# A seven-product pair for the first layer's last down chunks, and a new chunk order in the second mixer (Trainium2, one core)

## The chip, the cores and the metric

The kernel runs on one core of one Trainium2 chip. The metric is the device time of one execution in microseconds. The core's engines are TensorE (PE, with its weight loads as PEld), VectorE (DVE), ScalarE (ACT), GpSimd (POOL) and SyncE (SP), which here issues nearly all DMAs.

## The reference

A trunk of two layers on 256 tokens of width 2048 in float32. Each layer adds a token mixer and a gated MLP to the residual `h`, each behind an RMSNorm; a final RMSNorm closes it. Layer 0 mixes with a bidirectional mLSTM (8 heads), layer 1 with a bidirectional HGRN2 recurrence (16 heads of 128).

```python
for layer in range(DEPTH):
    hn = rmsnorm(h, norm_mix_g[layer])
    mix = mlstm_mixer(...) if layer % 2 == 0 else hgrn_mixer(...)
    h = h + mix
    h = h + conv_glu(rmsnorm(h, norm_ffn_g[layer]), ...)
return rmsnorm(h, final_g)

def conv_glu(hn, w_up, conv_w, conv_b, w_down):      # D_FF = 5504
    a, v = jnp.split(hn @ w_up, 2, axis=-1)
    c = conv_b + sum(ap[:, j:j + s] * conv_w[j] for j in range(3))   # ap: a padded by 1
    return (jax.nn.gelu(c, approximate=False) * v) @ w_down

# hgrn_mixer: q, i (the values V), g (the output gate), f_f, f_b = split(hn @ w_in)
```

## The kernel before

**Products.** Every float32 weight and activation is split into a high part, cast by ACT (L144), and a low part, subtracted by DVE (L145); each product is three matmuls (high by high, high by low, low by high). `split_weights` (L118) yields split pieces of 1024 weight columns; `stream` (L301) keeps three pieces ahead of the matmuls (`LOOK`).

**Chunks.** The kernel's work on PE is one list of `Chunk`s (L106), streamed in order. An "fm" chunk computes 256 features, features on the partitions (matmuls L340 of 512 columns and L344 of 256 for each k tile and half); `swap` exchanges the places of a 256-wide matmul and the 512-wide one behind it. A "tm" chunk computes 512 features with tokens on the partitions (six 512-wide matmuls of L356 for each k tile of 128). An "st" chunk is a **pair**: two 512-wide chunks of the down projection (or of a mixer's output projection) at once. It goes through its k tiles two at a time, a couple `u`. A couple plainly takes 2 x 2 x 2 products of 128x512, that is 24 matmuls (`squares_by_seven`, L214; all its matmuls are L231). A couple in `ch.seven` takes seven products, 21 matmuls, in the manner of Strassen: for this DVE forms three combinations T2, T3, T4 of the weight blocks and four sums of the token blocks (`token_sums`, L524). The pair uses all eight PSUM banks: four "mm" banks (pool psm) for the products that more than one block needs (P1, P6, P7, P5), four "aux" banks (pool psa) for the blocks themselves. After the last couple with seven, `mid` (L553 to L565) adds P1, P5, P6, P7 to the residual tile hm and so empties the psm banks; the couples behind it use the psa banks alone. `done` adds these at the end (four DVE adds).

**Weight combinations.** Those of a seven couple are either made when the piece is fetched (`combine`) or **stored**: `prepare` (L583) loads a couple's 1 MB as two 512 KB DMAs (`praw`), makes four DVE subtractions (L603), and stores it with two DMAs to DRAM (`tscr`). The pair later fetches 768 KB of the original (`raw`), 768 KB (`T`) and 256 KB from there. `prepare` runs as a side job during an earlier stage. `prepare_early` starts one in each mixer (`early[0]` in the first, period 19 for 8 items; `early[1]` in the second, period 26 for 15 items); each half of an FFN prepares others beside its up projection (`todo`). `ch.waits` holds a pair back, in program order, until its list of preparations is through.

**Order.** `Side` (L75) plans what runs beside the matmuls: generators that yield a delay in units of roughly a microsecond of PE work, which `stream` advances by `tick`. So the program order is fixed by hand when it is built: side jobs (preparation, norms, heads of the mixers) are put between the matmuls that tick past their due times. `late` issues a DMA on SP's queue pinned in program order.

**Stages.** Mixer 1 (`mlstm`), its output projection (`mixed`: a plain chunk, a pair with seven couples `SEVEN_MIX`, a plain chunk), FFN 0, mixer 2 (`hgrn`), its output projection, FFN 1. An FFN (`ffn`) goes in two parts of 22 and 21 feature tiles (FA, FB): up projection by "fm" chunks, gate and convolution by DVE and ACT, then the down projection of that part for all 2048 outputs, by two pairs. In part 0 both pairs have 8 seven couples (`SEVEN[0]`). In part 1 of layer 1 both have 7 (`SEVEN_END`). In part 1 of **layer 0** the first pair has 6 (`SEVEN[1]`), and the other two chunks are plain "tm" chunks (`project(...)[2:]`, weights `w_d2`).

**The seam.** While those plain chunks run, `Norm.add` and `Norm.turn` (L403 to L424) prepare the next norm: ACT squares each 512-wide quarter of hm, PE transposes it (L417, 16 transposes for the first two quarters) into an aux bank `pz`, and ACT and DVE split it into the activations `xt` (L362, L363). `turn` waits until no pair holds the banks (`held`). The last two quarters are turned after the last chunk. Then `hgrn` begins (`begin`, L938: the constant's DMA, the early preparation, small tables).

**Mixer 2.** For each quarter of 4 heads: three "fm" chunks, a V chunk ("tm"), three "fm" chunks, a G chunk ("tm", the output gate). A head's work (levels of products on ACT, DVE and POOL, then small PE products L1016, L1040, L1066) runs as a side job once its three "fm" results are there; it needs V for L1066, and its output needs G. V has one buffer.

Of the kernel before, what the change touches and what calls it, by code (L numbers as in the profile page):

```python
# [15 lines left out]
P = 128  # L16
# [30 lines left out]
LEAD = 48  # L47
TEMP = 3
GATES = 4 * AH
SEVEN = (1, 2, 3, 4, 6, 7, 8, 9), (1, 2, 4, 5, 7, 8)  # L50
SEVEN_END = (1, 2, 3, 4, 5, 6, 7)
END = 3
SCRATCH = 4096
SEVEN_MIX = (2, 4, 6)

QUAD = 32
LEVELS = (1, 2, 4, 8, 16, 32, 64)
FINE = 5
C_ID, C_MF, C_MB, C_SUM, C_LV = 0, 128, 384, 640, 768
# [1 line left out]


def trunk_kernel(ctx, tc, xT, x_d, fg_d, pp_d, cst_d, w_gate, w_first, w_aq, w_ak, w_av, w_ao, w_aout, w_ao2,
                 w_bq, w_bv, w_bg, w_bout, w_bo2, w_up, w_d0, w_d1, w_d2, w_d3, out, mscr, tscr):
    nc = tc.nc
    act, dve, pool, pe = nc.scalar, nc.vector, nc.gpsimd, nc.tensor

# [115 lines left out]
    def split_squares(ch, parts):  # L183

        units, raws, kept = (ch.nk + 1) // 2, {}, {}
        side.until(lambda: ch.waits is None or ch.waits)

        def raw(u):
            if u not in raws and u < units:
                n = 1536 if u in ch.stored else min(2048, 1024 * ch.nk - 2048 * u)  # L190
                raws[u] = load_raw(ch.src, 2048 * u, 2048 * u + n)
                if u in ch.stored:
                    kept[u] = temporary(ch.pool, "T")
                    nc.sync.dma_start(kept[u], ch.stored[u][:, 0:1536])
                    nc.sync.dma_start(raws[u][:, 1536:2048], ch.stored[u][:, 1536:2048])
            return raws.get(u)

        def combine(u):
            r, T = raw(u), temporary(ch.pool, "T")
            B11, B22, B21, B12 = (r[:, j * 512:(j + 1) * 512] for j in range(4))  # L200
            T2, T3, T4 = (T[:, j * 512:(j + 1) * 512] for j in range(3))
            for x, y, out in ((B12, B22, T3), (B12, B11, B12), (B22, B12, T2), (B21, T2, T4)):
                dve.tensor_tensor(out, x, y, ALU.subtract)
            kept[u] = T

        for u in range(units):
            r = raw(u)
            yield *parts(r[:, 0:1024], 1024, more=ch.pool), 1
            if u + 1 in ch.seven and u + 1 not in ch.stored:
                combine(u + 1)  # L210
            if u in ch.seven:
                yield *parts(kept[u][:, 0:1024], 1024, more=ch.pool), 1
            if 2 * u + 1 < ch.nk:
                yield *parts(r[:, 1024:2048], 1024, more=ch.pool), 1  # L214
            if u in ch.seven:
                yield *parts(kept[u][:, 1024:1536], 512, more=ch.pool), 1
# [4 lines left out]
    def squares_by_seven(ch, fetch, ready):  # L221
# [37 lines left out]
        for u in range(units):  # L259
# [27 lines left out]
            if u in ch.seven:  # L287
# [7 lines left out]
                products((C21, A22, T4))  # L295
                if u == last:
                    ch.mid(psm_)
                continue
            B21, B12 = piece()
            for ps, (x, w), (y, v) in ((C11, (A11, B11), (A12, B21)), (C12, (A11, B12), (A12, B22)),  # L300
# [80 lines left out]
    class Norm:  # L381
# [25 lines left out]

        def turn(self, c):
            yield 2.5
            while held:  # L410
                yield 1.0
            for k0 in (4 * c, 4 * c + 2):
                pz = aux("pz")
                for k in (k0, k0 + 1):
                    for t in range(2):
                        o = (k - k0) * T + t * P
                        pe.transpose(pz[:, o:o + P], hm[:, t, k * P:(k + 1) * P], ident)  # L417
                for k in (k0, k0 + 1):
                    self.take(k, pz[:, (k - k0) * T:(k - k0 + 1) * T])
                yield 1.0  # L420
# [127 lines left out]
    def pair(src, nk, c0, x, sums, norm, seven):  # L548
# [16 lines left out]
            pool.tensor_tensor(part(1, 1), part(1, 1), u, ALU.add)  # L565

        def done(ps):
            for i in range(4):
                h = part(i // 2, i % 2)
                dve.tensor_tensor(h, h, ps[i], ALU.add)  # L570
            if norm is not None:
                norm.add(c0)
                side.push(second())

        def second():
# [2 lines left out]

        ch = Chunk("st", src, nk, x, done)
        ch.mid, ch.seven, ch.sums = mid, seven, sums  # L580
        ch.stored, ch.waits, ch.pool = {}, None, None
        return ch

    def prepare(tiles, todo, first, period, finished, start, ahead):
# [66 lines left out]
    def mlstm(norm, nxt):  # L651
# [192 lines left out]
        for pr in range(AH // 2):  # L844
# [36 lines left out]
            def done_first(ps, done_v=done_v):  # L881
# [8 lines left out]
                norm.finish()  # L890
                done_v(ps, note)
                side.push(start(gs))
                prepare_early(box["mp"], 0, 45.0, 19.0)

            last = {}

# [32 lines left out]
    def hgrn(norm, nxt):  # L929
# [4 lines left out]
        def begin():  # L934
            mp = box["mp"] = stack.enter_context(tc.tile_pool(name="hg", bufs=1))
            late(cst[:, C_LV:], cst_d[:, C_LV:])
            prepare_early(mp, 1, 30.0, 26.0)
            box["turn"] = 0  # L938
            lb = box["lb"] = mp.tile([P, KT], F32, name="lb")
            oml = box["oml"] = mp.tile([P, KT], F32, name="oml")  # L940
# [147 lines left out]
                YT[hd] = slot(hd, "yb")  # L1088
                split(YT[hd], pz[:, 0:T], col("b_head_g", hd))

        swaps = {(0, 1): (0, 6), (1, 0): (2, 24), (1, 2): (4,), (2, 0): (2, 24), (2, 2): (4,), (3, 0): (2,), (3, 2): (10,)}
        heads = [dict() for _ in range(BH)]
        chunks = []
        for qd in range(BH // 4):
            four = dict()

# [5 lines left out]
            def done_g(ps, four=four, qd=qd):  # L1102
# [3 lines left out]
                    dve.scalar_tensor_tensor(sg[:, t], ps[t], norm.rc[:, t:t + 1], sg[:, t], ALU.mult, ALU.mult)  # L1106
                side.push(finish(qd, four))

            for i in range(6):
                if i == 3:  # L1110
                    chunks.append(Chunk("tm", w_bv[qd], KT, norm.x, done_v, paced=True))
                def done_i(ps, i=i, qd=qd):
                    for f in range(2):
                        r = 2 * i + f
                        take(4 * qd + r // 3, r % 3, ps[f])
                chunks.append(Chunk("fm", w_bq[6 * qd + i], KT, norm.x, done_i, begin if not chunks else None,
                                    swap=swaps.get((qd, i), (1, 13) if i == 3 else ()), paced=True))
            for j in range(4):
                heads[4 * qd + j]["qd"] = four
            chunks.append(Chunk("tm", w_bg[qd], KT, norm.x, done_g, paced=True))  # L1120

        def yx(k):
            side.until(lambda: YT[k] is not None)
# [5 lines left out]
    def ffn(layer, norm, nxt):  # L1129
        stack = ExitStack()  # L1130
        ending = isinstance(nxt, FinalNorm)
        seven = SEVEN[0], SEVEN_END if ending else SEVEN[1]
        box = dict(n=(2 * len(SEVEN[0]) + len(SEVEN[1])) * layer)
        chunks, pairs = [], []

        def begin():
# [7 lines left out]
        def done_up(f, i, GT, SX, seven):  # L1144
            def go(ps):
# [17 lines left out]
                GT.append(g)  # L1163
                if i % 2 and i // 2 in seven:
                    n = seven.index(i // 2)
                    if seven is not SEVEN[1]:
                        z = GT[i - 1][:, P:T], GT[i - 1][:, T + P:2 * T]
                    else:
                        if n % 3 == 0:
                            box["s4"] = mp.tile([P, 768], F32R, tag=f"sx{len(seven) + n // 3}", name="s4")  # L1170
                        z = tuple(box["s4"][:, (n % 3 * 2 + j) * P:(n % 3 * 2 + j + 1) * P] for j in range(2))
                    SX[i // 2] = token_sums(mp, n, box["c"], c, avc[:, 0:2 * T], z)
                box["c"] = c
            return go
# [1 line left out]
        for part, (f0, nf) in enumerate(((0, FA), (FA, FB))):  # L1176
# [7 lines left out]
                                  todo, 18.0, (nf * 10.4 - 26.0) / len(todo), finished, late, True))  # L1184

            for i in range(nf):
                chunks.append(Chunk("fm", w_up[layer, f0 + i], KT, norm.x, done_up(f0 + i, i, GT, SX, seven[part]),
                                    prep if i == 0 else None,
                                    swap=(2,) if part and i == 0 else (3,) if f0 + i == 1 else (), paced=True))
            def two(src, c0, norm, seven, todo=todo, finished=finished, GT=GT, SX=SX, nf=nf):  # L1190
                ch = pair(src, nf, c0, lambda k: GT[k], lambda u: SX[u], norm, seven)
                for u in seven:
                    ch.stored[u] = tscr[box["n"]]
                    todo.append((src[:, 2048 * u:2048 * (u + 1)], tscr[box["n"]]))
                    box["n"] += 1
                ch.waits, ch.pool = finished, None
                pairs.append(ch)
                return ch

            chunks.append(two(w_d0[layer][:, f0 * 1024:(f0 + nf) * 1024], 0, nxt if part else None, seven[part],  # L1200
                              *(() if part else early[layer])))
            if not part:
                chunks.append(two(w_d1[layer], 2, None, seven[0]))
            elif ending:
                chunks[-1].before = nxt.load
                chunks.append(two(w_d3, 2, None, seven[1], *early[layer]))
                chunks[-1].last, chunks[-1].half = True, nxt.half
            else:
                chunks += project(lambda c: w_d2[c % 2], nf, lambda k, GT=GT: GT[k], nxt)[2:]
        return chunks, stack.close  # L1210


# [54 lines left out]
def layout(x, norm_mix_g, norm_ffn_g, mlstm_w_in, mlstm_b_gate, mlstm_head_g, mlstm_w_out, hgrn_w_in, hgrn_lb,  # L1267
# [16 lines left out]
    def outer(w):  # L1284
# [21 lines left out]
        w_bv=_cols(wb[:, 2048:4096], 512), w_bg=_cols(wb[:, 4096:6144], 512),  # L1306
        w_up=np.ascontiguousarray(up).reshape(2, FT, P, KT * 256),
        w_d0=np.stack([squares(d[:, :, 0:2]) for d in down]), w_d1=np.stack([squares(d[:FA, :, 2:4]) for d in down]),
        w_d2=np.ascontiguousarray(down[0, FA:, :, 2:].transpose(2, 1, 0, 3)).reshape(2, P, FB * 512),
        w_d3=squares(down[1, FA:, :, 2:]),  # L1310
    )


def build(nc, ins, out_shape=(2, P, D), **kw):
# [1 line left out]
          for k, a in ins.items()}  # L1316
    out = nc.dram_tensor("out", out_shape, F32, kind="ExternalOutput").ap()
    mscr = nc.dram_tensor("mscr", (64, T), F32, kind="Internal").ap()
    tscr = nc.dram_tensor("tscr", (4 * len(SEVEN[0]) + len(SEVEN[1]) + 2 * len(SEVEN_END), P, 2048), F32, kind="Internal").ap()
    with tile.TileContext(nc, schedule_with_timeline_sim=True) as tc:  # L1320
        with ExitStack() as ctx:
            trunk_kernel(ctx, tc, ap["xT"], ap["x"], ap["fg"], ap["pp"], ap["cst"], ap["w_gate"], ap["w_first"],
                         ap["w_aq"], ap["w_ak"], ap["w_av"],
                         ap["w_ao"], ap["w_aout"], ap["w_ao2"], ap["w_bq"], ap["w_bv"], ap["w_bg"],
                         ap["w_bout"], ap["w_bo2"], ap["w_up"], ap["w_d0"], ap["w_d1"], ap["w_d2"], ap["w_d3"], out, mscr, tscr, **kw)


# [10 lines left out]
```

## Time and profile before

| | us |
| --- | --- |
| median of 3 runs | 2383.42 |
| lowest and highest | 2383.26, 2383.58 |
| the profiled run | 2384.87 |
| its span in the trace | 2382.9 |

The span runs from the first instruction to the last one's end; the run's time also holds what lies around it. Stages in the trace, in us from the span's start: mixer 1 to 303 and its output projection to 395; FFN 0 up to 637, its two pairs to 735, up to 979, the pair to 1032.5, the two plain chunks to 1092; mixer 2 to 1592 and its output projection to 1683; FFN 1 to 2373. In the rows a group is "line engine operation out<-in xcount"; in a timeline the first number is the start and the second the time from there to the end of the last of the group.

### The profile page before, as it was taken

How to read it: one execution, taken by the hardware profiler on the slowest of the kernel's cores; microseconds unless marked ns; L12 is line 12 of the kernel's file. 1: busy time of each engine (PE TensorE's matmuls, PEld its weight loads, DVE VectorE, ACT ScalarE, POOL GpSimd, SP SyncE). 2: the span in 40 equal slices, each digit the busy share in tenths (PEclk: the TensorE clock that was granted, in tenths of full speed). 3: DMA queues.
4: the chain of work that ended last, by engine and by line, in shares of the span. 5: the costliest groups of instructions: out<-in, count | busy, mean ns of one | idle time of the engine just before them, and what ended most of it. 6: DMA issues, size and time to landing. Idle time of an engine off the chain costs nothing.

```text
span 2382.9 us, 38182 instructions
## 1 busy us (share of the span) xinstructions
PE 2365.6 (99%) x14572; PEld 2024.3 (85%) x14572; DVE 1938.4 (81%) x3001; ACT 1433.6 (60%) x2271; POOL 205.4 (9%) x242
## 2 busy tenths in 40 slices
PE   9999999999999999999999999999999999999998
PEld 7888888888888888888888888887888888888886
DVE  7777687888788887766888888888788788888787
ACT  7655456555665555655666666665555566455565
POOL 0100000000000000001233222320000000000000
PEclk9999999999999999999999999999999999999999
DMA  8777656886697885755666666764788588887695
GB/s 300 240 272 268 227 174 214 302 303 226 223 354 272 283 280 195 274 190 204 244 234 228 246 236 227 245 225 173 258 299 283 195 309 310 288 288 253 204 345 201
DMA packets 112471, 601.23 MB, mean 252 GB/s; under 512 B 12688, under 2 KB 13200, under 8 KB 66464
## 3 DMA queue, kind: packets, MB, share of 16 engines
q1 hardware_dynamic: 110592, 594.78, 71.1%
q0 software_dynamic: 1120, 3.21, 0.8%
q8 instruction: 114, 1.87, 0.3%
q10 hardware_dynamic: 576, 0.79, 0.1%
q14 instruction: 69, 0.57, 0.1%
HBM read 542.05 MB, written 56.69 MB: 251 GB/s over the span
## 4 chain that ended last, share of the span: by engine, by line
PE 95%; DVE 2%; DMA 1%; issue 1%; ACT 0%; SPq 0%; POOL 0%; DVEq 0%; POOLq 0%; ACTq 0%
PE mm L340 36%; PE mm L356 18%; PE mm L344 18%; PE pc L231 12%; PE mm L231 6%; DMA praw<-in_w_d 1%; PE py L1066 1%; PE pn L808 1%; DVE wl L145 1%; PE pd L1016 0%; PE pz L417 0%; PE pa L1016 0%; DVE QK L1029 0%; DMA Mb<-mscr 0%; DMA raw<-in_w_first 0%
## 5 line engine op out<-in xcount | busy, mean ns | idle before, releaser
L340 PE MATMUL mm<-xt,wh 128*128 128x512 f32 x3776 | 1314.2, 394 | 0.0
L145 DVE TENSOR_TENSOR wl<-raw,wh 128x1024 fp32r<-128x1024 f32 (+1 forms) x845 | 1034.6, 1229 | 274.6 <-ACT wh L144 268.9
L144 ACT CAST wh<-raw 128x1024 fp32r<-128x1024 f32 (+1 forms) x845 | 875.6, 1042 | 520.4 <-PE mm L340 293.6
L344 PE MATMUL mm<-xt,wl 128*128 128x256 f32 x3776 | 1046.3, 278 | 0.0
L340 PEld LDWEIGHTS mm<-xt,wh 128*128 128x128 f32 x3776 | 706.2, 188 | 160.1
L344 PEld LDWEIGHTS mm<-xt,wl 128*128 128x128 f32 x3776 | 709.7, 188 | 4.5 <-issue 0.4
L356 PE MATMUL mm<-wh,xt 128*128 128x512 f32 x1024 | 320.5, 391 | 2.2 <-ACT xt L362 1.6
L231 PE MATMUL pc<-wh,g 128*128 128x512 f32 x676 | 228.0, 389 | 0.0
L356 PEld LDWEIGHTS mm<-wh,xt 128*128 128x128 f32 x1024 | 191.1, 188 | 41.8 <-ACT xt L362 2.0
L356 PE MATMUL mm<-wl,xt 128*128 128x512 f32 x512 | 197.9, 391 | 0.0
L603 DVE TENSOR_TENSOR praw<-praw 128x512 f32<-128x512 f32 x208 | 143.8, 691 | 49.4 <-DMA praw<-in_w_d 39.0
L231 PEld LDWEIGHTS pc<-wh,g 128*128 128x128 f32 x676 | 126.9, 188 | 26.4
L231 PE MATMUL pc<-wl,g 128*128 128x512 f32 x338 | 131.5, 389 | 0.0
L145 DVE TENSOR_TENSOR wl<-T,wh 128x1024 fp32r<-128x1024 f32 (+1 forms) x116 | 110.2, 961 | 20.2 <-ACT wh L144 19.5
L231 PE MATMUL mm<-wh,sx 128*128 128x512 f32 x348 | 124.4, 391 | 0.0
L144 ACT CAST wh<-T 128x1024 fp32r<-128x1024 f32 (+1 forms) x116 | 96.2, 836 | 45.8 <-PE pc L231 20.3
L564 POOL TENSOR_TENSOR hm<-hm,u 128x512 f32<-128x512 f32 x9 | 12.6, 1395 | 1186.4 <-DVE u L563 592.3
L1029 DVE TENSOR_TENSOR QK<-QK,G 128x256 f32<-128x256 f32 x224 | 109.7, 537 | 5.4 <-ACT kq L1008 5.0
L356 PEld LDWEIGHTS mm<-wl,xt 128*128 128x128 f32 x512 | 96.2, 188 | 19.1
L1150 ACT COPY avc<-mm 128x256 f32<-128x256 f32 x172 | 64.2, 373 | 78.2 <-PE mm L344 78.2
L1008 ACT COPY kq<-QK 128x512 f32<-128x512 f32 x112 | 74.5, 669 | 57.3 <-DVE QK L1029 44.6
L1151 DVE TENSOR_TENSOR avc<-mm,avc 128x256 f32<-128x256 f32 x172 | 71.9, 418 | 12.7 <-ACT avc L1150 12.6
(247 smaller groups left out, 2322.3 us busy)
## 6 DMA issues: line engine op xcount, KB each, us to landing
raw<-in_w_up SPq DMA_DIRECT2D x172, 1024.0 KB, 5.4
praw<-in_w_d SPq DMA_DIRECT2D x104, 512.0 KB, 6.8
tscr<-praw SPq DMA_DIRECT2D x104, 512.0 KB, 6.8
raw<-in_w_bq SPq DMA_DIRECT2D x48, 1024.0 KB, 5.0
raw<-in_w_d SPq DMA_DIRECT2D x52, 768.0 KB, 6.1
T<-tscr SPq DMA_DIRECT2D x52, 768.0 KB, 7.7
raw<-in_w_d SPq DMA_DIRECT2D x32, 1024.0 KB, 5.2
raw<-in_w_ao SPq DMA_DIRECT2D x24, 1024.0 KB, 4.9
```

Source lines behind the costliest of these rows:

```text
L144: pin(act.copy(wh[:, :m], r))
L145: pin(dve.tensor_tensor(wl[:, :m], r, wh[:, :m].bitcast(F32), ALU.subtract))
L231: pe.matmul(ps, a, b, start=id(ps) not in begun, stop=stop and i == 2)
L340: pe.matmul(ps[f], wh[:, c:c + P], x, start=k + kk == 0, stop=False)
L344: pe.matmul(ps[f][:, 0:T], wl[:, c:c + P], x[:, 0:T], start=False, stop=k + kk == ch.nk - 1)
L356: pe.matmul(ps[t], x[:, a + t * P:a + (t + 1) * P], w[:, c], start=st and i == 0, stop=sp and i == 2)
L603: dve.tensor_tensor(out, x, y, ALU.subtract)
L808: pe.matmul(pn[:, 0:258], w, v, start=(i == 0), stop=(i == len(parts) - 1))
L1008: act.copy(m, blocks(QK, h))
L1029: dve.tensor_tensor(two[:, j], two[:, j], by[:, j], ALU.mult)
L1150: act.copy(z, p[:, T:2 * T])
L1151: dve.tensor_tensor(z, p[:, 0:T], z, ALU.add)
```

## The change

1. `SEVEN[1]` becomes (1, ..., 7) for both layers and `SEVEN_END` goes. In layer 0's part 1 the first pair thus has seven seven-product couples, and the two plain chunks become a second pair (`w_d3[0]`) with seven.
2. `EARLY = 4` of this new pair's seven couples are prepared in mixer 1 (12 items at a period of 13), the other three beside part 1's up projection (10 items instead of 6). `waits` is now a list of such lists.
3. The last pair is marked `ends`: once `mid` has been issued, `rest` is set, and `Norm.turn` may go on although the pair holds the aux banks; it then transposes into psm banks. `done` goes quarter by quarter, with the norm's squares of the first between.
4. In mixer 2 the chunks are laid out anew: V of the first quarter comes first, then the other V and G chunks alternate before the "fm" chunks numbered in `TMS`; the last G comes last. Every "fm" chunk gets two swaps. The early preparation there has period 20 instead of 26.

```diff
-SEVEN = (1, 2, 3, 4, 6, 7, 8, 9), (1, 2, 4, 5, 7, 8)
-SEVEN_END = (1, 2, 3, 4, 5, 6, 7)
+SEVEN = (1, 2, 3, 4, 6, 7, 8, 9), (1, 2, 3, 4, 5, 6, 7)
+EARLY = 4
+TMS = (0, 4, 8, 11, 15, 18, 21)
...
-        side.until(lambda: ch.waits is None or ch.waits)
+        side.until(lambda: all(ch.waits))
...
                 if u == last:
                     ch.mid(psm_)
+                    ch.rest = ch.ends
...
         def turn(self, c):
             yield 2.5
-            while held:
+            while held and not held[-1].rest:
                 yield 1.0
             for k0 in (4 * c, 4 * c + 2):
-                pz = aux("pz")
+                pz = psm.tile([P, 512], F32, tag="mm", name="pz") if held else aux("pz")
...
         def done(ps):
-            for i in range(4):
-                h = part(i // 2, i % 2)
-                dve.tensor_tensor(h, h, ps[i], ALU.add)
+            for c in range(2):
+                for t in range(2):
+                    h = part(t, c)
+                    dve.tensor_tensor(h, h, ps[2 * t + c], ALU.add)
+                if norm is not None and c == 0:
+                    norm.add(c0)
             if norm is not None:
-                norm.add(c0)
                 side.push(second())
...
-                prepare_early(box["mp"], 0, 45.0, 19.0)
+                prepare_early(box["mp"], 0, 45.0, 13.0)
...
-            prepare_early(mp, 1, 30.0, 26.0)
+            prepare_early(mp, 1, 30.0, 20.0)
...
-        swaps = {(0, 1): (0, 6), (1, 0): (2, 24), (1, 2): (4,), (2, 0): (2, 24), (2, 2): (4,), (3, 0): (2,), (3, 2): (10,)}
...
+            vs.append(Chunk("tm", w_bv[qd], KT, norm.x, done_v, begin if qd == 0 else None, paced=True))
+            gs.append(Chunk("tm", w_bg[qd], KT, norm.x, done_g, paced=True))
             for i in range(6):
-                if i == 3:
-                    chunks.append(Chunk("tm", w_bv[qd], KT, norm.x, done_v, paced=True))
...
-                chunks.append(Chunk("fm", w_bq[6 * qd + i], KT, norm.x, done_i, begin if not chunks else None,
-                                    swap=swaps.get((qd, i), (1, 13) if i == 3 else ()), paced=True))
+                n = 6 * qd + i
+                fs.append(Chunk("fm", w_bq[n], KT, norm.x, done_i, swap=(2, 13) if n in TMS else (4, 15), paced=True))
...
-            chunks.append(Chunk("tm", w_bg[qd], KT, norm.x, done_g, paced=True))
+        for n, ch in enumerate(fs):
+            if n in TMS:
+                i = TMS.index(n)
+                chunks.append((vs, gs)[i % 2][i // 2])
+            chunks.append(ch)
+        chunks.append(gs[3])
...
-                ch.waits, ch.pool = finished, None
+                    (early[layer][0] if i < first else todo).append((src[:, 2048 * u:2048 * (u + 1)], tscr[box["n"]]))
+                if first:
+                    ch.waits = [early[layer][1]] + [finished] * (first < len(seven))
...
-            else:
-                chunks += project(lambda c: w_d2[c % 2], nf, lambda k, GT=GT: GT[k], nxt)[2:]
+            chunks.append(two(w1, 2, nxt if part and not ending else None, SEVEN[part],
+                              0 if not part else len(SEVEN[1]) if ending else EARLY))
...
+                else:
+                    chunks[-1].ends = True
```

## Prediction before the run

> **What bounds the kernel now.** I read the page first: its span, busy shares and chain of waits.
>
> ```profile
> span 2382.9 us, 38182 instructions
> PE 2365.6 (99%) x14572; PEld 2024.3 (85%) x14572; DVE 1938.4 (81%) x3001; ACT 1433.6 (60%) x2271; POOL 205.4 (9%) x242
> PE 95%; DVE 2%; DMA 1%; issue 1%; ACT 0%; SPq 0%; POOL 0%; DVEq 0%; POOLq 0%; ACTq 0%
> ```
>
> PE is busy for 2365.6 of 2382.9 us and makes 95% of the chain. Only 17.3 us are idle, so time leaves mainly with PE instructions. Next, the waits of PE and the edges of the span (in windows the columns are stretch, sum, then busy time of PE, PEld, DVE, ACT, POOL, granted clock, DMA share, GB/s).
>
> ```profile
> PE pc L231 <- ACT wh L144: 1.8, 2, 1.6
> PE pd L1016 <- issue: 0.7, 1, 0.7
> PE pn L808 <- DVE y L816: 0.7, 1, 0.7
> PE py L1066 <- ACT V L1100: 0.2, 1, 0.2
> ...
> 0.00:4.00 4.00, 2.90 (x132) 2.90 (x136) 0.00 (x0) 1.28 (x1) 0.68 (x8) 1.00 0.54 146
> 4.00:12.00 8.00, 5.79 (x79) 4.24 (x72) 4.54 (x9) 4.86 (x10) 0.00 (x0) 1.00 1.02 362
> 2373.00:2383.00 10.00, 0.00 (x0) 0.00 (x0) 4.16 (x9) 2.35 (x5) 0.56 (x1) 0.66 0.58 210
> ```
>
> Start and end hold 1.1 + 2.2 + 10.0 = 13.3 us of the idle time, and the change touches neither. Inside the kernel 4.0 us are left; the largest wait (L231) lies in the second mixer's output projection. A busy PE can also be slow, and there it was:
>
> ```profile
> 1632.90:1635.60 2.70, 0.94 (x3) 0.30 (x2) 2.70 (x5) 2.03 (x3) 0.00 (x0) 1.00 0.01 3
> 1635.60:1639.00 3.40, 3.38 (x8) 2.55 (x9) 3.40 (x5) 2.85 (x4) 0.00 (x0) 0.50 0.31 51
> ```
>
> PE idled 2.70 - 0.94 = 1.8 us in the first stretch; in the second its granted clock was 0.50.
>
> **The change, part by part.**
>
> *Matmuls of the down projection.* Price of a 128x512 matmul from PE's timeline (start, time from first start to last end), first in the plain chunks that go (L356, with transposes at L417), then where orders are swapped (L340), then in a couple of a pair (L231):
>
> ```profile
> 1038.46 0.60 PE L417 MATMUL pz<-cst,hm 128*128 128x128 f32 x4
> ...
> 1039.13 0.39 PE L356 MATMUL mm<-wl,g 128*128 128x512 f32 x1
> ...
> 1040.04 0.62 PE L356 MATMUL mm<-wh,g 128*128 128x512 f32 x2
> ...
> 1041.40 0.39 PE L356 MATMUL mm<-wh,g 128*128 128x512 f32 x1
> ...
> 1151.76 0.63 PE L340 MATMUL mm<-xt,wh 128*128 128x512 f32 x2
> ...
> 1152.46 0.40 PE L340 MATMUL mm<-xt,wh 128*128 128x512 f32 x1
> ...
> 1153.15 0.40 PE L340 MATMUL mm<-xt,wh 128*128 128x512 f32 x1
> ...
> 2286.01 0.39 PE L231 MATMUL mm<-wh,g 128*128 128x512 f32 x1
> ...
> 2289.86 0.39 PE L231 MATMUL mm<-wl,sx 128*128 128x512 f32 x1
> ```
>
> From 1040.04 to 1041.40 starts advance by six matmuls, 0.227 us each; from 2286.01 to 2289.86 by 17 (first and last shown), 0.226 each. One price, set by the rate of starts and not by the 0.39 of one. A couple of two k tiles costs 24 matmuls plainly and 21 with seven products. The last two chunks had none with seven and get 7: 21 fewer. The pair before them goes from 6 to 7: 3 fewer. The built programs agree: 252 matmuls at L356 go, 228 at L231 come, all other PE counts are equal. 24 x 0.227 = **5.44 us off the path**. The swaps inside "fm" chunks add no matmul: four took 0.70 us with one (1151.76 to 1152.46) and 0.69 without (to 1153.15); 30 more swaps are 0.3 us at the most, I take 0.
>
> *Vector work that comes with it.* Eight more stored couples mean 8 more preparations of four L603 subtractions, 8 more splits of each T form, 7 adds and sums for one more pair, and one more token sum.
>
> ```profile
> L603 DVE TENSOR_TENSOR praw<-praw 128x512 f32<-128x512 f32 x208 | 143.8, 691 | 49.4 <-DMA praw<-in_w_d 39.0 <-issue 9.8
> L145 DVE TENSOR_TENSOR wl<-T,wh 128x1024 fp32r<-128x1024 f32 x58 | 70.7, 1219 | 19.3 <-ACT wh L144 18.9
> L145 DVE TENSOR_TENSOR wl<-T,wh 128x512 fp32r<-128x512 f32 x58 | 40.7, 702 | 0.9 <-ACT wh L144 0.6
> ...
> 120.00:300.00 180.00, 180.00 (x939) 153.94 (x938) 132.13 (x239) 99.17 (x161) 7.43 (x8) 1.00 0.74 253
> 420.00:640.00 220.00, 220.00 (x1269) 192.27 (x1268) 184.56 (x298) 124.06 (x197) 0.00 (x0) 1.00 0.76 266
> 750.00:960.00 210.00, 210.00 (x1214) 183.64 (x1213) 171.40 (x266) 114.16 (x180) 0.00 (x0) 1.00 0.74 251
> 1110.00:1590.00 480.00, 479.09 (x4365) 412.84 (x4364) 413.59 (x704) 327.57 (x618) 146.39 (x174) 1.00 0.68 237
> 2276.00:2320.00 44.00, 44.00 (x195) 36.42 (x194) 39.98 (x41) 30.54 (x33) 3.54 (x2) 1.00 0.93 341
> ```
>
> 208 subtractions are 52 preparations; one is 4 x 0.691 + 49.4/52 of waiting = 3.7 us of DVE. Four more go to the first mixer (120 to 300: 73% busy, then at most 147 of 180, 82%), four more to the up projection's second part (750 to 960: 82%, then 171.4 + 4 x 3.7 + some 2 for sums = 188 of 210, 90%). PE ran unbroken beside DVE at 184.6/220 = 84% (420 to 640) and at 40.0/44 = 91% (2276 to 2320), so I take 0; if that cover goes, the bound is one waiting preparation per stage, 2 x 3.7 = 7.4 us. DVE's other neighbours have room: ACT, with 16 more casts, is busy 60%. In the second mixer the same 15 preparations come every 20 instead of every 26 units: 3.7/20 instead of 3.7/26 is 4% more DVE beside 86%, for the 15 x 20 units that they then take. I take 0 with a bound of +3.7.
>
> *Transfers.* Each stored couple fetches 768 + 768 + 256 KB.
>
> ```profile
> raw<-in_w_d SPq DMA_DIRECT2D x52, 768.0 KB, 6.1
> T<-tscr SPq DMA_DIRECT2D x52, 768.0 KB, 7.7
> raw<-tscr SPq DMA_DIRECT2D x52, 256.0 KB, 6.7
> ...
> 2290.00:2300.00 10.00, 10.00 (x46) 8.29 (x45) 9.21 (x9) 7.89 (x9) 0.00 (x0) 1.00 1.00 389
> ```
>
> The queue of SP (SyncE), which issues these, gets 47 more (16 loads and 16 stores of preparations, 8 + 8 returns, one load fewer), and later weight loads stand behind stores that wait for DVE, as they did 104 times before. Both pairs now have the form that the second layer's pairs have already (seven couples in a row of 10 1/2). There, 2276 to 2320, the DMA was at 0.93, for ten of those us at 1.00, and PE lost nothing. So 0; the price if they starve is a rival.
>
> *The seam to the second mixer.* Sixteen transposes move into the last pair and its end; their number stays. The first eight now wait on PE's queue for banks that open as DVE reads the seventh couple's sums, and behind them stand the pair's last couples. The second layer's first pair shows the same sums without the transposes:
>
> ```profile
> 2304.07 0.68 DVE L558 TENSOR_TENSOR hm<-hm,mm 128x512 f32<-128x512 f32 x1
> ...
> 2311.61 0.68 DVE L563 TENSOR_TENSOR u<-u,mm 128x512 f32<-128x512 f32 x1
> 2313.07 5.07 DVE L145 TENSOR_TENSOR wl<-raw,wh 128x1024 fp32r<-128x1024 f32 x3 [0.79 <-ACT wh L144]
> ...
> L564 POOL TENSOR_TENSOR hm<-hm,u 128x512 f32<-128x512 f32 x9 | 12.6, 1395 | 1186.4 <-DVE u L563 592.3 <-PE mm L231 297.8 <-ACT wh L144 296.3
> L363 DVE SCALAR_TENSOR_TENSOR xt<-pz,pp,xt 128x256 fp32r<-128x256 f32 x48 | 21.4, 478 | 3.3 <-ACT xt L362 3.2
> ```
>
> From the first sum to the end of three splits DVE took 2318.1 - 2304.1 = 14.0 us, 0.8 of it waiting for casts, so it was ahead. PE has 60 matmuls there, 13.6 us, plus now 12 transposes: four and one matmul took 1039.13 - 1038.46 = 0.67, so 0.44 per four and 1.3 in all. The last bank opens with L563, 2312.3 - 2304.1 = 8.2 us after the first sum; its transposes stand 46 matmuls, 10.4 us, in. DVE gets 8 splits (L363) more, 3.8 us: it ends 17.8 after instead of 14.9, 2.9 us late. What hides that is the lead: weights are split three pieces ahead (LOOK), and a piece of 12 matmuls is 2.7 us. The third and fourth quarters of the activations come after the last matmul. The V chunk, first now, needs x tile 8 after 48 matmuls and 8 transposes, 10.9 + 0.9 = 11.8 us; four adds, three weight splits and the split at L363 are 4 x 0.68 + 3 x 1.7 + 0.5 = 8.3 of DVE. A former first "fm" k tile is 1536 columns wide against 3072, so tile 8 would be due in half the time. The setup ahead of the chunk is the same and issues the same one DMA on SP; on ACT one exponential and on POOL two adds (L564) are queued there, 1.4 us each. I take 0, bound +2.9.
>
> If such a late DVE stops PE for 2 us, the rows at 1632.9 say that half clock may follow: 8 matmuls in 3.4 us instead of 1.8, 1.6 us more. [...]
>
> *The stop at 1632.9.* In the built program DVE still has the same eight weight splits, then sums and six combining subtractions, between the last head's transposes and the next split. So it stays: 0.
>
> **Sum.** On the profiled execution: 2382.9 - 5.4 = 2377.5 of span; its run was 2384.87, 1.97 outside the span and 1.45 above the median of the runs, 2383.42. The saving is in PE work, so I take it from the median: 2383.42 - 5.44 = **2378.0**.
>
> **Rivals.** (a) *Better: the stop shrinks.* Its 6.1 us hold 11 matmuls, 2.5 us worth, so 3.6 are lost, of which half clock is 1.6. The sequence on PE is slightly different and falls differently in time. Without half clock 2376.4, without the stop 2374.4. For: the idle time is just over half of 2.7 us. Against: the same DVE work stands ahead. (b) *Part is given back:* at the seam (2.9, with half clock 4.5), or in the second mixer (3.7), where DVE at 86% and denser preparations delay heads: between half of the smaller and both, 2378.0 + 1.5 to 6.6 = 2379.5 to 2384.6. For: PE waited there for a head's V and y. Against: those waits were 0.2 to 0.7 us, and V first removes the former. [...] (c) *Slower: the two pairs starve for data.* Seven couples of 1.84 MB, three of 1.05 and a half make 16.5 MB in 231 matmuls, 52.4 us: 315 GB/s, twice in a row. At nine tenths of that, 284, each pair takes 58.1, together 11.4 more: 2389.4. The whole gain is lost below 299 GB/s. Against: 341 GB/s in the same form at 2276. That fewer matmuls are not issued is excluded by the counts.
>
> **Chances.** Forecast (2376.6 to 2379.5) 0.45; (a) 0.20; (b) 0.25; (c) 0.10. The range runs from 2374.0, the stop gone, to 2384.6, the end of (b); it leaves out (c), a little of (a) and the 7.4 of waiting preparations, together under 0.2. 0.2%, about what a measurement tells from no change, is 4.77 us, so faster means under 2378.65: (a) 0.20 and three quarters of the forecast, 0.34, make 0.54. Slower is over 2388.2, in (c) under 287 GB/s: 0.08. Same: 0.38.
>
> **What would show it.** L356's line with 252 matmuls fewer and L231's with 228 more, PE about 5.4 us less busy; no PE wait at L417 and L356 between 1030 and 1110 (seam); DVE near 90% and PE unbroken from 750 to 960; DMA near 0.93 and PE unbroken in both pairs; the wait at L231 for casts again at about 1632.9 - 5.4 = 1627.5. The forecast is wrong if PE waits at the seam or in heads for over 1.5 us, if a second half-clock stretch appears, or if the old one is gone.

## The result, and the profile after

The changed kernel takes **2389.21 us** (median of 9 runs, 2385.38 to 2391.24), the kernel before 2383.5 in as many runs (2382.31 to 2385.84). The ratio is 1.0023, 95% interval 1.0013 to 1.0033. The forecast was 2378.0, in a range from 2374.0 to 2384.6. From the page of the changed kernel (a run of 2391.24): span, busy time, and the shares of the chain of waits.

```profile
span 2388.9 us, 38320 instructions
PE 2367.0 (99%) x14548; PEld 2019.7 (85%) x14548; DVE 1972.0 (83%) x3060; ACT 1442.5 (60%) x2289; POOL 217.3 (9%) x244
PE 85%; DMA 7%; DVE 5%; issue 2%; ACT 1%; POOL 0%; SPq 0%; DVEq 0%; POOLq 0%; ACTq 0%
```

PE has 14572 - 14548 = 24 instructions fewer, as forecast, and yet is busy for 1.4 us more: matmuls were slower. DMA's share of the chain went from 1% to 7%: something on the path now waits for transfers. The waits of PE (engine, line waited for: us, times, longest), the largest ones:

```profile
PE py L1070 <- ACT AT L1059: 2.1, 1, 2.1
PE pz L840 <- DVE y L835: 1.6, 2, 0.9
PE pc L232 <- ACT wh L145: 1.6, 3, 1.0
PE pn L812 <- DVE Wl L804: 1.4, 2, 1.1
...
PE pn L812 <- DVE y L820: 0.7, 1, 0.7
PE pn L812 <- ACT Wh L803: 0.6, 1, 0.6
```

L812 and L840 are head products of the first mixer, L1070 one of the second. The time by stages, from the starts of the first "fm" matmul of each in PE's timeline (before L340, after L342); the last two columns belong to experiments below:

| stage, us more than before | changed | e9 | e10 |
| --- | --- | --- | --- |
| up to the first "fm" matmul | -1.4 | -0.2 | +1.8 |
| mixer 1 and its output projection | +6.2 | +0.3 | -1.2 |
| FFN 0, part 0 | 0.0 | 0.0 | 0.0 |
| FFN 0, up projection of part 1 | +2.3 | 0.0 | 0.0 |
| its pairs, mixer 2, output projection | -1.9 | -5.2 | -0.6 |
| FFN 1, to the last matmul | +0.9 | 0.0 | 0.0 |
| sum | +6.0 | -5.1 | +0.1 |

(Rounding leaves 0.1 in two of the sums.) The table compares single executions: the profiled run of the changed kernel was 2.0 us above its median, that of the kernel before 1.4 above its own. The first row holds nothing that the change touches. The losses too vary in one and the same code. In the profiled runs of e4, e6 and e7, whose code is the changed kernel's in the first mixer, that row was +7.7, +2.6 and +3.2; in those of e1, e3, e4, e6 and e8, whose code is the changed kernel's in the up projection of part 1, that row was 0.0, +0.2, +0.7, 0.0 and +2.6.

So the pair's saving is there, but in this run 6.2 us are lost in a stage of which the forecast said 0. There DVE waits; the waits of DVE for `praw`, the tiles of the preparations, in the first mixer (30 to 300), before and then after:

```profile
DVE praw L603 <- DMA praw<-in_w_d: 6.7, 5, 2.5
```

```profile
DVE praw L607 <- DMA praw<-in_w_d: 28.3, 10, 5.4
DVE praw L607 <- issue: 8.5, 2, 5.6
```

36.8 us instead of 6.7. The queue of SP tells why. Its waits for stores in that mixer (60 to 280), before and after:

```profile
SPq L378 <- DMA tscr<-praw: 0.4, 1, 0.4
```

```profile
SPq L380 <- DMA tscr<-praw: 27.9, 13, 5.2
```

A preparation loads a tile, changes it, stores it, and the next load of the same tile has to wait until the store has landed. One round of it, on SP's timeline and on DVE's (start, duration):

```profile
203.44 0.33 SPq L610 DMA_DIRECT2D tscr<-praw  x1
...
205.18 0.33 SPq L610 DMA_DIRECT2D tscr<-praw  x1
...
208.63 4.71 SPq L380 DMA_DIRECT2D praw<-in_w_d  x2
```

```profile
218.89 0.69 DVE L607 TENSOR_TENSOR praw<-praw 128x512 f32<-128x512 f32 x1 [2.27 <-DMA praw<-in_w_d]
```

The second store is issued at 205.2. The load's second half is held on SP until 213.0, when that store has landed, and DVE, which comes to the subtraction at 216.6, waits 2.3 us with everything that is queued behind it. PE was not stopped by this round. It was by others, as at 295.6, where a head's weights (`Wl`) stand behind the late subtraction:

```profile
295.62 0.69 DVE L607 TENSOR_TENSOR praw<-praw 128x512 f32<-128x512 f32 x1 [3.62 <-DMA praw<-in_w_d]
296.24 0.95 DVE L804 TENSOR_TENSOR Wl<-W,Wh 128x768 fp32r<-128x768 f32 x1
```

```profile
297.24 0.51 PE L812 MATMUL pn<-Vh,Wl 128*128 128x258 f32 x2 [1.13 <-DVE Wl L804]
```

### The profile page after: what moved, and what is told of

It is laid out like the page before. It is cut to its first block, busy times and chain, and to the rows that moved or that the text cites. A ratio compares the mean times of both kernels' runs of the same rounds, so it can differ in the third digit from the quotient of the medians.

```text
span 2388.9 us, 38320 instructions
## 1 busy us (share of the span) xinstructions
PE 2367.0 (99%) x14548; PEld 2019.7 (85%) x14548; DVE 1972.0 (83%) x3060; ACT 1442.5 (60%) x2289; POOL 217.3 (9%) x244
## 3 DMA queue, kind: packets, MB, share of 16 engines
q0 software_dynamic: 1120, 3.21, 0.7%
## 4 chain that ended last, share of the span: by engine, by line
PE 85%; DMA 7%; DVE 5%; issue 2%; ACT 1%; POOL 0%; SPq 0%; DVEq 0%; POOLq 0%; ACTq 0%
PE mm L342 32%; PE mm L346 16%; PE mm L358 14%; PE pc L232 13%; PE mm L232 7%; DMA praw<-in_w_d 4%; DVE wl L146 2%; DMA tscr<-praw 1%; DVE praw L607 1%; PE py L1070 1%; PE pd L1020 0%; PE pz L419 0%; PE pa L1020 0%; ACT wh L145 0%; DMA T<-tscr 0%
## 5 line engine op out<-in xcount | busy, mean ns | idle before, releaser
L342 PE MATMUL mm<-xt,wh 128*128 128x512 f32 x3776 | 1313.5, 394 | 0.1
L342 PEld LDWEIGHTS mm<-xt,wh 128*128 128x128 f32 x3776 | 705.7, 188 | 160.5 <-issue 0.2
L232 PE MATMUL pc<-wh,g 128*128 128x512 f32 x776 | 260.9, 390 | 0.2 <-ACT wh L145 0.2
L607 DVE TENSOR_TENSOR praw<-praw 128x512 f32<-128x512 f32 x240 | 167.2, 697 | 80.6 <-DMA praw<-in_w_d 63.7
L232 PEld LDWEIGHTS pc<-wh,g 128*128 128x128 f32 x776 | 145.6, 188 | 30.9 <-ACT wh L145 0.6
L232 PE MATMUL pc<-wl,g 128*128 128x512 f32 x388 | 150.9, 389 | 0.0
L232 PE MATMUL mm<-wh,sx 128*128 128x512 f32 x396 | 140.2, 390 | 0.5 <-ACT wh L145 0.4
L146 DVE TENSOR_TENSOR wl<-T,wh 128x512 fp32r<-128x512 f32 (+1 forms) x132 | 124.0, 953 | 20.1 <-ACT wh L145 19.6
L145 ACT CAST wh<-T 128x512 fp32r<-128x512 f32 (+1 forms) x132 | 109.6, 835 | 38.7 <-PE pc L232 14.1
L232 PEld LDWEIGHTS mm<-wh,sx 128*128 128x128 f32 x396 | 74.2, 188 | 16.6 <-ACT wh L145 1.3
```

The costliest lines, as they stand in the source:

```text
L145: pin(act.copy(wh[:, :m], r))
L146: pin(dve.tensor_tensor(wl[:, :m], r, wh[:, :m].bitcast(F32), ALU.subtract))
L232: pe.matmul(ps, a, b, start=id(ps) not in begun, stop=stop and i == 2)
L342: pe.matmul(ps[f], wh[:, c:c + P], x, start=k + kk == 0, stop=False)
```

## Two theories

**Round trip.** A preparation's tiles need a store and a load before they can be worked on again: 6.4 + 7.0 us to landing, by these rows of the page after (KB each, median us to landing):

```profile
praw<-in_w_d SPq DMA_DIRECT2D x120, 512.0 KB, 7.0
tscr<-praw SPq DMA_DIRECT2D x120, 512.0 KB, 6.4
```

The plan leaves a third of the period to the store and half of it to the load: at 19 units 6.3 + 9.5, at 13 units 4.3 + 6.5 = 10.8. By this theory the first subtraction of a preparation reaches the head of DVE's queue before its data, and the loss comes of *when* the loads are asked for.

**Amount.** The twelve preparations are simply more DVE work (4 x 3.7 us) in a mixer whose heads bear no delay, and the loss comes of *how much* there is.

## The experiments

All were timed against the kernel before on the same chip, whose median there was 2383.8 to 2384.1; beside the changed kernel's 2389.21 it was 2383.5, so differences to 2389.21 are uncertain by the 0.3 to 0.6 us between the two.

**e5: the short period alone, in the kernel before.**

```diff
-                prepare_early(box["mp"], 0, 45.0, 19.0)
+                prepare_early(box["mp"], 0, 45.0, 13.0)
```

> The kernel before with one number changed: the 8 early preparations of the first mixer come at a period of 13 units instead of 19; their number stays 8. Theory 1 (round trip): a preparation's tiles are stored, then loaded anew; stores take 6.4 us and loads 6.6 in the trace, 13.0 together, while a period of 13 leaves 13/3 + 13/2 = 10.8 for both, so the first subtraction of each waits at the head of DVE's queue. DVE then waits for praw about 8/12 of the 36.8 us seen in the changed kernel, some 25 us (before: 6.7), and PE loses about 8/12 of 6.2 = 4 us in the first mixer: 2387.5. Theory 2 (amount): the four additional preparations crowd DVE, whatever their period; then nothing is lost here: 2383.5, and DVE's waits stay under 10 us.

Measured: 2387.2 (ratio 1.0014, 1.0005 to 1.0023), 3.1 us more. DVE's waits for praw in the first mixer:

```profile
DVE praw L603 <- DMA praw<-in_w_d: 13.7, 6, 3.6
DVE praw L603 <- issue: 7.8, 2, 4.9
```

21.5 us instead of 6.7, with no preparation added. The amount theory falls for this part.

**e1: a longer period in the changed kernel.**

```diff
-                prepare_early(box["mp"], 0, 45.0, 13.0)
+                prepare_early(box["mp"], 0, 30.0, 17.5)
```

> The changed kernel with its 12 early preparations of the first mixer at a period of 17.5 from 30 on instead of 13 from 45 on. Theory 1 (round trip): 5.8 units for the store and 8.8 for the load cover most of 6.4 + 6.6 us; DVE's waits for praw in the first mixer fall from 36.8 to under 15 us, and the mixer gets back 4 to 6 of the 6.2 us: 2383 to 2385. Theory 2 (amount): as many preparations, so as much is lost: 2388 to 2390.

Measured: 2393.01 (1.0039, 1.0026 to 1.0052), against both expectations. The heads did get their time back: up to the last "fm" matmul the mixer is 0.4 us shorter than before, against 4.0 longer in the changed kernel. But the last preparation now came at 325, in the output projection, and DVE then waited 7.3 us for its store to land before it went on:

```profile
339.19 0.69 DVE L204 TENSOR_TENSOR T<-raw 128x512 f32<-128x512 f32 x1 [7.30 <-DMA tscr<-praw]
```

PE stood there, and was slow afterwards (windows: stretch, sum, PE, PEld, DVE, ACT, POOL, granted clock, DMA share, GB/s):

```profile
335.70:342.30 6.60, 0.38 (x2) 0.00 (x0) 3.11 (x9) 1.06 (x2) 0.00 (x0) 0.77 0.18 71
342.30:345.50 3.20, 2.14 (x4) 1.32 (x5) 3.20 (x6) 3.20 (x4) 0.00 (x0) 0.50 0.20 28
345.50:349.20 3.70, 3.70 (x10) 2.72 (x10) 3.70 (x6) 0.68 (x2) 0.00 (x0) 0.50 0.64 259
```

From the last "fm" matmul to the FFN, which is mostly the output projection, 12.7 us were lost. So twelve preparations from 30 on at a period that bears the round trip do not fit; my expectation had the mechanism and not the room.

**e3: the first mixer's preparations as before; the new pair has three seven couples instead of seven.** Four of its couples then multiply token blocks that already hold sums, so that the products are not the reference's, but the number and shape of the matmuls are those of plain couples.

```diff
-EARLY = 4
+EARLY = 0
...
-                prepare_early(box["mp"], 0, 45.0, 13.0)
+                prepare_early(box["mp"], 0, 45.0, 19.0)
...
-            chunks.append(two(w1, 2, nxt if part and not ending else None, SEVEN[part],
+            chunks.append(two(w1, 2, nxt if part and not ending else None, SEVEN[part] if not part or ending else SEVEN[part][4:],
```

> The changed kernel with the first mixer's preparations as before (8 at a period of 19): the new pair has only the three seven-product couples that are prepared beside the up projection, so four couples cost 24 matmuls instead of 21, 12 x 0.227 = 2.7 us more. By theories 1 and 2 the first mixer gives back its 6.2 us: 2389.2 - 6.2 + 2.7 = 2385.7, with the second mixer's stop and the up projection's 2.3 us still there. If the first mixer's time has another cause than the preparations: 2391.9.

Measured: 2392.23 (1.0032, 1.002 to 1.0045). The total missed; the stages did not. From the first "fm" matmul to the FFN the first mixer took 362.4 us (before 362.6, changed 368.8). From the end of part 1's up projection to the second mixer's first "fm" matmul it took 133.8, the changed kernel 131.1: 2.7 us for four couples, as forecast, so a seven couple is worth 3 x 0.227. What hid it: 4.4 us more in the second layer's first up projection, where nothing waited (PE was busy for 252.00 of 252.00 us from 1683 to 1935, at a granted clock of 1.00), and a stop in the second output projection (+1.2; the longest wait of PE in that run is 2.5 us, at L232). The first led to e11.

**e4: second mixer as before** (old order, old swaps, period 26; the rest as changed).

> The changed kernel with the second mixer as before: old chunk order, old swaps, period 26. If the stop of 2.26 us at 1260 and the half clock behind it (1.6) come of the new order and period, they go: 2389.2 - 3.9 = 2385.3, if the seam bears the old order. Rival: the seam needs the new order, since the first fm chunk asks for x tile 8 in half the time; then PE waits at the seam for 2 to 5 us and the time stays at 2387 to 2390.

Measured: 2385.38 (1.0006, 0.9997 to 1.0015; 11 runs), 3.8 below the changed kernel, as expected. The seam bears the old order too: one wait of 0.3 us at 1102. The run took order, swaps and period back together.

**e6: new order, old period.**

```diff
-            prepare_early(mp, 1, 30.0, 20.0)
+            prepare_early(mp, 1, 30.0, 26.0)
```

> The changed kernel with its new chunk order, but the second mixer's early preparations at the old period of 26 instead of 20. If the stop at 1260 and the half clock behind it (3.9 us) come of the denser preparations, they go: about 2385.3. If they come of the new order, in which a head's last product and V stand where a preparation's wait happens to fall, a stop of 1 to 3 us appears there or at another head: 2387 to 2390. In the order alone the sum of DVE's waits for praw in this mixer, 11.1 us after against 11.5 before, speaks for the second.

Measured: 2388.9 (1.002, 1.0011 to 1.0028; 11 runs from 2383.41 to 2392.86). By the medians the longer period alone gives nothing back, so with e4 the new order, together with its swaps, is left. The profiled run was the fastest of the eleven (2383.41), and in it the stop at 1260 has shrunk to 0.2 us while one of 1.5 us stands at another head product, as the second expectation had it:

```profile
PE pd L1020 <- issue: 1.5, 1, 1.5
PE py L1070 <- ACT AT L1059: 0.2, 1, 0.2
```

From the end of part 1's up projection to FFN 1 even this run took 2.5 us more than e9. The swaps themselves are not where the time goes: in the second mixer a 512-wide start and the 256-wide one behind it take 0.3533 us together in e9, which has the old swaps, and 0.3539 in e10, which has the new ones, 0.4 us over some 720 such pairs.

**e7: the up projections' preparations over their whole period.**

```diff
+            yield period / 3
             if not ahead:
-                yield period / 3
                 load(i + 1)
```

> The changed kernel with the preparations beside the up projections spread over the whole of their period (now they take two thirds of it: 17 us each in the first layer's second part). Theory 1 (a load asked for too late, so that DVE stands at the head of its queue): DVE's waits for praw from 735 to 990 fall from 13.1 us to under 5, the 2.3 us lost there go, the rest stays: 2386.9. Theory 2 (ten preparations are too much work for DVE): the 2.3 us stay: 2389.2.

Measured: 2386.97 (1.0013, 1.0004 to 1.0022), 2.2 below the changed kernel, but the two intervals overlap. DVE's waits for praw from 735 to 990, in the changed kernel and then here:

```profile
DVE praw L607 <- DMA praw<-in_w_d: 13.1, 6, 4.7
```

```profile
DVE praw L607 <- DMA praw<-in_w_d: 2.6, 7, 0.6
```

The stage is as long as before (232.6 us). Ten preparations are not too much work; they came too close upon each other. But a late load does not always reach PE: in the profiled runs of e1 and e6, whose code is the changed kernel's here, DVE waited 12.1 and 12.0 us and the stage took 232.6 us all the same.

**e8: the first mixer's preparations from 15 on, at 16.**

```diff
-                prepare_early(box["mp"], 0, 45.0, 13.0)
+                prepare_early(box["mp"], 0, 15.0, 16.0)
```

> The changed kernel with the 12 early preparations of the first mixer starting at 15 instead of 45 and at a period of 16 instead of 13, so that the last still ends ahead of the output projection's pair (e1 ran over into it). Theory 1 (round trip): the first mixer gives back 5 to 6 us, like e1's mixer, and nothing is late behind it: 2383.5 to 2385. Theory 2 (amount): no gain, 2388 to 2390.

Measured: 2385.17 (1.0005, 0.9996 to 1.0014), 4.0 below the changed kernel with as many preparations. DVE's waits for praw in that mixer:

```profile
DVE praw L607 <- DMA praw<-in_w_d: 2.7, 3, 1.9
```

36.8 us became 2.7. The amount theory falls here too.

**e9: e7, e8 and the second mixer of before together.**

> The changed kernel with all three: preparations of the first mixer from 15 on at 16, those of the up projections spread, and the second mixer's old order, swaps and period. If the pair saves its 24 matmuls and everything else that was lost is due to preparations and the new order: 2378.0 (2377 to 2380). If the pair or the transposes in its banks cost something of their own: 2381 or more.

Measured: **2379.85** (0.9986, 0.9978 to 0.9995; 11 runs from 2378.29 to 2382.93), faster than both kernels. In its profile the last matmul starts 5.1 us earlier than before, against 5.44 forecast; by the medians it gains 3.9 us (the interval of the ratio makes that 1.2 to 5.2). Undone one at a time, the three losses came to 4.0 (e8), 2.2 (e7) and 3.8 (e4), and together to 9.4. From its page:

```profile
span 2377.8 us, 38332 instructions
PE 2358.7 (99%) x14548; PEld 2019.5 (85%) x14548; DVE 1978.4 (83%) x3060; ACT 1444.1 (61%) x2289; POOL 210.6 (9%) x244
```

DVE is as busy as in the changed kernel (1978.4 and 1972.0 us), and PE needs 8.3 us less for the same number of matmuls.

**e10: e9 with the new second mixer.**

> The same as e9, but with the changed kernel's second mixer (V first, new swaps, period 20). Theory: the new order costs by itself what e4 and the traces show, a stop of about 2 us at a head's last product at 1255 and slow matmuls behind it, 3 to 4 us against e9: 2379.9 + 3.5 = 2383.4. Rival: the stop came of delays from the first mixer and goes with them: 2380.

Measured: 2383.22 (1.0000, 0.9991 to 1.0009): the new order and its swaps and period cost 3.4 us without delays from the first mixer. The stop is at the same place (L1070, 2.4 us).

**e12: control, the kernel before with e9's cures and without the pair.**

> Control: the kernel before with e9's two cures alone (first mixer's 8 preparations from 15 on at 22, those of the up projections spread), without the pair. DVE's waits for praw go there too (6.7 and 1.4 us), but PE waited for little of them: 2383 to 2384, so that e9's gain is the pair's. If the cures are worth as much without the pair: 2380.

Measured: 2383.7 (0.9999, 0.999 to 1.0008). So e9's gain is the pair's.

**e13: e9 without transposes in the free banks.**

```diff
-            while held and not held[-1].rest:
+            while held:
```

> e9 with the transposes of the last pair waiting until the pair has left all banks, as they did for other pairs, instead of going into the banks that its seventh couple leaves. What the use of the free banks is worth: x tile 0 then comes after the last matmul, behind four adds (2.7 us), transposes and splits, some 5 us in which PE has little to do: 2379.9 + 4 to 6 = 2384 to 2386. If it is worth nothing: 2380.

Measured: 2383.56 (0.9997, 0.9988 to 1.0006), 3.7 above e9. The waits of PE from 1030 to 1120:

```profile
PE mm L342 <- DVE xt L365: 1.6, 2, 0.9
PE pz L419 <- DVE hm L573: 1.1, 1, 1.1
```

In e9 there is one of 0.3 us. Its profiled run is 5.1 us longer than e9's: 2.1 of these lie at the seam and in the mixer behind it, 1.7 in the first mixer and 1.3 in other pairs, where both kernels have the same code. So the banks are worth 2 to 4 us.

**e11: the kernel before without one swap of two matmuls per layer.**

```diff
-                                    swap=(2,) if part and i == 0 else (3,) if f0 + i == 1 else (), paced=True))
+                                    swap=(2,) if part and i == 0 else (), paced=True))
```

> The kernel before without one swap of two matmuls, in the second fm chunk of each layer's first up projection. In the traces a 512-wide and a 256-wide matmul together take 0.3467 us in nearly all up projections, but 0.3532 all through one (e3, layer 1) and from a 0.5 us wait to the end of the stage in another (changed kernel, from 910). If a wait or a swap sets a rhythm that lasts to the end of the stage, this kernel falls into the slower one in the first parts: up to 2 x 20 chunks x 0.21 = 8.4 us more, 2392; in one of the two, 2388. If the rhythm has nothing to do with the swap: 2383.8.

Measured: 2392.91 (1.0037, 1.0024 to 1.0049), 8.9 more. The first up projection of each layer took 249.67 instead of 245.22 us. The same 100 us of it, in the kernel before and in e11 (windows):

```profile
460.00:560.00 100.00, 100.00 (x579) 87.43 (x578) 86.05 (x143) 56.23 (x90) 0.00 (x0) 1.00 0.83 295
```

```profile
460.00:560.00 100.00, 100.00 (x568) 86.74 (x568) 85.29 (x140) 54.77 (x86) 0.00 (x0) 1.00 0.83 286
```

PE never stands still, the granted clock is 1.00 in both, and 568 matmuls fall in it instead of 579.

## Why the prediction was wrong, point by point

- **24 matmuls, 5.44 us off the path: right.** The count is on the page, four couples cost 2.7 us (e3), and with the losses removed the stage that holds the pair is 5.2 us shorter in the trace (e9), while the cures alone bring nothing (e12). The medians show 3.9 of the 5.44.
- **"so I take 0 ... the bound is one waiting preparation per stage": the step that failed.** I priced preparations by DVE's busy time and by the mean wait of the trace of before, 49.4/52 us, and asked whether PE runs beside a DVE at 84 or 91%. It does: DVE's total was never the limit (e8; e9, where it is busy for 1978.4 us against 1972.0). What changed was the period, 19 to 13, and beside the up projection six items to ten. The rows to see it stood on the page of before:

```profile
praw<-in_w_d SPq DMA_DIRECT2D x104, 512.0 KB, 6.8
tscr<-praw SPq DMA_DIRECT2D x104, 512.0 KB, 6.8
```

  That is 13.6 us for store and load, against 13/3 + 13/2 = 10.8 units (a unit is roughly a microsecond). Measured: 6.2 and 2.3 us in the profiled run (2.6 to 7.7 and 0 to 2.6 over the runs of the same code), where the forecast had 0 and a bound of 7.4 that entered neither the sum nor the range. That the preparations cost it is shown by e5, e8 and e9; for the 2.3 us it is less sure, since they come in some runs only.
- **The second mixer, "0 with a bound of +3.7": the size of the bound, and another mechanism.** I feared the density. DVE's waits for praw did not rise there (10.4 + 0.7 us after, 9.8 + 1.7 before), and the longer period gives nothing back (e6). With the new order one wait stands ahead of a head's masks, for which its last product on PE is due. DVE, ACT and PE in the changed kernel:

```profile
1259.86 0.69 DVE L607 TENSOR_TENSOR praw<-praw 128x512 f32<-128x512 f32 x1 [3.55 <-DMA praw<-in_w_d]
1260.47 0.22 DVE L1055 COPY_PREDICATED AD<-cst,pd 128x64 f32<-128x64 int32 x1
```

```profile
1261.85 1.00 ACT L1059 COPY AT<-AD 32x64 f32<-32x64 f32 x4 [3.93 <-DVE AD L1055]
```

```profile
1262.91 1.16 PE L1070 MATMUL py<-V,AT 128*128 128x128 f32 x8 [2.10 <-ACT AT L1059]
```

  PE stood for 2.1 us and then had a granted clock of 0.54 for 3.4 us:

```profile
1264.00:1267.40 3.40, 3.40 (x10) 2.62 (x9) 3.40 (x7) 2.47 (x4) 0.00 (x0) 0.54 0.74 271
```

  No run kept the new order without these waits, so what the order costs alone is not shown. "V first removes the former" was right (PE no longer waits for V at that product) and did not matter. The half clock after a stop of 2 us was foreseen, but put at the seam.
- **The seam, 0: right.** PE waits nowhere between 1030 and 1120 in the changed kernel, and giving up the banks costs 2 to 4 us (e13).
- **Transfers, 0 for the pairs, rival (c): right that they don't starve.** From 979 to 1092 PE is busy 113.00 of 113.00 us at 305 GB/s. The late transfers were elsewhere: in the first mixer, loads held back until a store had landed (27.9 us on SP's queue).
- **The stop at 1632.9, "So it stays: 0": right in sum, wrong in kind.** From the last "fm" matmul of the mixer to FFN 1 the kernel took 0.3 us less. The stop did not stay: between 1592 and 1683 PE waited four times, at most 1.0 us and 2.8 in all, at a granted clock of 1.00. That the half clock hangs on which share of a stretch PE idles, as rival (a) takes it, was my estimate; no run shows it.
- **Rival (b), part given back:** the right kind, with a cap of 6.6 us; by the profiled runs 11.4 were given back (6.0 more instead of 5.4 less), most of it in the stage that had no rival.

The remaining 0.9 us lie in the second layer's last pairs. There (2276 to 2290) ACT waited for one transfer in the changed kernel, and four matmuls between 2284.3 and 2286.1 start 0.9 us late in sum; in e9, whose code is the same there, PE waited for nothing. Why the transfer came late is open:

```profile
ACT wh L145 <- DMA T<-tscr: 3.7, 1, 3.7
```

Why the runs of the kernels with late loads scatter more (e6: 9.5 us over 11 runs, the kernel before on the same chip 3.9 over 33) is shown in part only. The same code lost different times in the same stage (beside the table by stages), and a stop was followed by the slow rhythm of e11 for the rest of a stage in one run (below); that these two make up the scatter is argued.

## What to carry to other kernels

Before a buffer is turned over faster, add up its round trip (store to landing, load to landing, work) and compare it with the new period (here 13.6 us for store and load against 10.8); an average of busy time or of waits at the old period (here 49.4/52 us) did not show it. The price of a late load was not the wait of the engine that needs it but that of the work queued behind it there: 36.8 us of DVE's waits went with 6.2 us lost in the first mixer, and 12.1 us beside the up projection in e1 with none. A change of several parts can hold a real gain: undo the parts one at a time, and run the control with the cures alone.

## What the hardware showed unexpectedly

A steady stream of alternating 512-wide and 256-wide matmuls ran in two rhythms here: 0.3467 us for a pair of them (mean over 667 pairs of part 1's up projection, kernel before) and 0.3534 (e11, 697 pairs; e3 0.3533). One swap of two matmuls near the start decided it in e11. In the changed kernel the change came with a stop: the up projection of part 1 took 10.75 us for a chunk (first to last 512-wide start) until a matmul was held back by 0.6 us at 910, and 10.95 for each of the six chunks behind the one with the stop; 1.2 of the 2.3 us lost there are this. In e3 the slow rhythm held from the start of the second layer's first up projection, in code that is the same as before; what set it is not shown. No wait and no clock shows the rhythm (the granted clock was 1.00 in both), only the count of matmuls in a window (579 and 568 in 100 us).

A stop of 2.1 us in the changed kernel was followed by a granted clock of 0.54, while in e9 the clock stayed at 1.00 behind one of 2.3 us:

```profile
86.00:89.00 3.00, 0.68 (x4) 0.29 (x4) 2.07 (x6) 2.99 (x4) 0.00 (x0) 1.00 0.99 87
89.00:92.50 3.50, 3.50 (x23) 3.11 (x23) 3.50 (x6) 3.19 (x4) 0.00 (x0) 1.00 0.90 283
```

In the kernel before, 1.8 us of idle time (1632.9 to 1635.6) were followed by a granted clock of 0.50 (1635.6 to 1639.0). So the length of a stop alone did not decide it; what else did is not shown.
